# Up projection turned on VectorE in 32x32 blocks and regrouped by transfers, in place of TensorE transposes

## The chip, the cores and the metric

The kernel runs on one core of a Trainium2 chip. The metric is the time of one execution in device microseconds (us). Engines are named as in the profile: PE is TensorE (matrix products), PEld its weight load, DVE VectorE, ACT ScalarE, POOL GpSimd, SP SyncE, which only issues transfers here.

## The reference, cut to what matters

One decoder layer on 256 tokens of width 2048 in float32: parallel mixers, cross attention, and at its end a gated MLP with a causal convolution of width 3 over the tokens, then a last norm. The change touches only the MLP's first half:

```python
def causal_depthwise_conv(u, w, bias):      # per column c: y[s] = w0 u[s-2] + w1 u[s-1] + w2 u[s] + bias
    ...
def conv_ffn(h, w_up, conv_w, conv_b, w_down):
    u = causal_depthwise_conv(h @ w_up, conv_w, conv_b)
    gate, val = u[..., :D_FF], u[..., D_FF:]
    return (jax.nn.silu(gate) * val) @ w_down      # D_FF = 5632
```

## The kernel before

**Products.** Activations are held transposed and split into a high and a low part, and so are the weights. `product` computes one unit, 512 columns of x @ w for both blocks of 128 tokens, into two PSUM tiles. Weights come in transfers of 1 MB (four 128-row blocks) that SP issues into three buffers. Each is worked off in two half blocks of 256 rows: ACT casts the half block to its high part (`_hi`, L162), DVE subtracts for the low part (`_lo`, L163), and PE runs 12 matmuls of 128x512 (two row blocks, two token blocks, three terms: L168 hi x hi, L169 hi x lo, L170 lo x hi). There are three buffers each for the high and low parts, so the cast of a half block waits for the matmuls of the third half block before it. A unit of the up projection (2048 rows) is eight half blocks, 96 matmuls. After each half block `tick` lets waiting tasks go on: a task is a generator, started by `spawn(gen, delay)`, which yields the number of half blocks to let pass.

**Up stage.** 22 units, each with 256 gate and 256 value columns. After a unit ACT takes the two PSUM tiles to SBUF, scaled by the norm factor of each token (L588, `zu`). Two half blocks later `gated` runs: for the gate and for the value part PE transposes four 128x128 blocks into a PSUM tile (L562, `uT`), eight in all for a unit; for each of the four 128-column blocks ACT makes the tap of the token itself and the bias (L568) and DVE adds the other two taps (L570, L572); then a sigmoid (L576), two multiplications (L577, L578) and the split into the tile `gT` (L117, L118) that the down projection reads. Tiles that live long (`x2T`, `xr`, `gT`) share a pool of 34 buffers (`b4`).

**Order.** The code is emitted in the order of the loops, and a scheduler puts the instructions of PE, ACT, DVE and POOL in order, each engine's list being fixed when the kernel is built; SP's list stays as written. Each engine works its list off strictly in order. In the up stage POOL has nothing to do.

Of the kernel before, what the change touches and what calls it, by code (L numbers as in the profile page):

```python
# [16 lines left out]
P = 128  # L17
S = 256          # tokens
NT = S // P      # token blocks
D = 2048  # L20
KD = D // P      # 128-row blocks of the model width
FF = 5632
KF = FF // P
U = 512          # columns of one product unit
KB = 4           # 128-row blocks per weight transfer
# [6 lines left out]
# columns of the packed per-partition parameters  # L32
# [13 lines left out]
def hybrid_layer(ctx: ExitStack, tc: tile.TileContext, x, xT, mem, memT, gmix, par, gfin,  # L46
# [28 lines left out]
    # additive masks of the diagonal blocks: [q, k] -> 0 where k <= q (k < q), else NEG  # L75
# [8 lines left out]
    # Work that is emitted between the products: generators that yield the number of  # L84
    # half blocks of weights to let pass before they go on.
# [27 lines left out]
    def split(dst, src, gains=None):  # L113
        """dst[:, 0] + dst[:, 1] = src, or src * gain, in two parts of 12 bits.
        dst [P, 2, 2, S], src [P, 2, S]; gains: a [P, 1] column per 128-row block."""
        if gains is None:
            nc.scalar.copy(out=dst[:, 0], in_=src)  # L117
            nc.vector.tensor_tensor(out=dst[:, 1], in0=src, in1=dst[:, 0].bitcast(F32),  # L118
                                    op=ALU.subtract)
            return  # L120
        for j in range(2):
            nc.scalar.activation(out=dst[:, 0, j], in_=src[:, j], func=AF.Copy, scale=gains[j])
            nc.vector.scalar_tensor_tensor(out=dst[:, 1, j], in0=src[:, j], scalar=gains[j],
                                           in1=dst[:, 0, j].bitcast(F32),
                                           op0=ALU.mult, op1=ALU.subtract)

    def transposed(dst, src, n, name, gains=None):
        """dst: act tiles of the 4 row blocks n*4.. of the transpose; src [P, NT, U]."""
        for h in range(2):
            pt = sm_tile(f"{name}_tp").rearrange("p (j s) -> p j s", j=2)  # L130
            for j in range(2):
                for t in range(NT):
                    c = (2 * h + j) * P
                    nc.tensor.transpose(out=pt[:, j, t * P:(t + 1) * P],
                                        in_=src[:, t, c:c + P], identity=ident)
            k0 = 4 * n + 2 * h
            dst[k0 // 2] = act_tile(f"{name}_{h}")
            split(dst[k0 // 2], pt, None if gains is None else [gains(k0), gains(k0 + 1)])
        yield 0
# [5 lines left out]
    def rstd(ss, n, width, name):  # L145
        """(sum over the last axis of ss [P, n, m] / width + EPS) ** -0.5 -> [P, n]"""
        tot = st.tile([P, n], F32, name=f"{name}_t", tag="st_t")
        nc.vector.tensor_reduce(out=tot, in_=ss, op=ALU.add, axis=AX)
        nc.vector.tensor_scalar(out=tot, in0=tot, scalar1=1.0 / width, scalar2=EPS,
                                op0=ALU.mult, op1=ALU.add)  # L150
        r = st.tile([P, n], F32, name=name, tag=name, bufs=1)
        nc.gpsimd.tensor_tensor(out=r, in0=tot, in1=mhalf[:, :n], op=ALU.pow)
        return r
# [12 lines left out]
    def mm3(out, a, b, start=True, stop=True):  # L166
        """out (+)= (a[0] + a[1]).T @ (b[0] + b[1]) without the product of the two low parts."""
        nc.tensor.matmul(out, lhsT=a[0], rhs=b[0], start=start, stop=False)  # L168
        nc.tensor.matmul(out, lhsT=a[0], rhs=b[1], start=False, stop=False)  # L169
        nc.tensor.matmul(out, lhsT=a[1], rhs=b[0], start=False, stop=stop)  # L170
# [6 lines left out]
    def product(xs, w, u, kt_n, name, pieces=None, before=None, heap=False):  # L177
        """x @ w[:, unit u] for both token blocks -> two PSUM tiles [P, U].
        pieces: 128-row blocks per transfer; before(kt): called ahead of the transfer from kt on."""
        ps = [ps_mm.tile([P, U], F32, tag="mm", name=f"{name}_mm{t}") for t in range(NT)]  # L180
        k0 = 0
        for n in pieces or [KB] * (kt_n // KB):
            if before:
                before(k0)
            if heap:
                raw = chunk_tile(f"{name}_raw", [P, 2, U])[:, 0:n, :]
            else:
                raw = wr_p.tile([P, KB, U], F32, tag="raw", name=f"{name}_raw")[:, 0:n, :]
            k4 = k0 % KB
            nc.sync.dma_start(out=raw, in_=w[u, k0 // KB].rearrange("p (k c) -> p k c", k=KB)[:, k4:k4 + n])  # L190
            for h in range(0, n, 2):
                m = min(2, n - h)
                hi, lo = split_w(raw[:, h:h + m, :], m,
                                 ws_p.tile([P, 2, U], F32R, tag="whi", name=f"{name}_hi"),
                                 ws_p.tile([P, 2, U], F32R, tag="wlo", name=f"{name}_lo"))
                for j in range(m):
                    kt = k0 + h + j
                    for t in range(NT):
                        multiply(ps[t], xs, hi, lo, kt, j, t, kt == kt_n - 1)
                if (k0 + h) % 2 == 0 or m == 1 and kt % 2:  # L200
                    tick()
            k0 += n
        return ps

    def load_split(src, gains, i, name):
        """Split act tile i of a transposed input [P, KD, S] in DRAM, scaled by gains."""
# [27 lines left out]
    def proj_T2(ps, r, name):  # L234
        """Evacuate a unit scaled by r and transpose it: act tiles of heads 0, 1 and 2, 3."""
# [7 lines left out]
    def proj_T(ps, r, name, rotate=False):  # L243
        """Evacuate a unit scaled by r and transpose it: [P (dim), 4 (head), S]."""
# [21 lines left out]
    def proj_n(ps, r, name):  # L266
        """Evacuate a unit scaled by r: [P (token), NT, U]."""
# [5 lines left out]
    def attn_T(a, name):  # L273
        """Causal weights of one head [q block][P, K] -> [P (key), 3 * P]:
        keys 0 for both query blocks, then keys 1 for query block 1."""
# [8 lines left out]
    # differential attention  # L284
    oaT = [None] * 4

    def diff_head(h):
        qT, kT, v, hh = qa[h // 4], ka[h // 4], va[h // 4], h % 4
        # scores of the two maps, in a bank each: query block 0 in 0:P, query block 1 in P:3 * P
# [62 lines left out]
    # stick-breaking attention, two heads at a time  # L352
    obT = [None] * 4

    def stick_pair(g):
        aw = [[], []]
        for i in range(NT):
# [14 lines left out]
            # softplus(z) = max(z, 0) + ln(1 + exp(-|z|)), zero where masked  # L372
# [27 lines left out]
    # the input projection in units; the attention of a group of heads runs between the products  # L400
# [21 lines left out]
    # lam = exp(q1.k1) - exp(q2.k2) + LAM_INIT, negated, on all partitions  # L422
# [33 lines left out]
    # branch projections, gated and merged  # L456
# [18 lines left out]
    # output projection and residual  # L475
# [77 lines left out]
    gT = [None] * (KF // 2)  # L553

    def gated(i, z):
        us = []
        for part in range(2):          # gate, value
            pt = sm_tile("uT").rearrange("p (j s) -> p j s", j=2)
            for j in range(2):
                for t in range(NT):  # L560
                    c = (2 * part + j) * P
                    nc.tensor.transpose(out=pt[:, j, t * P:(t + 1) * P], in_=z[t][:, c:c + P],  # L562
                                        identity=ident)
            u = wk.tile([P, 2, S], F32, tag="w2", name="u")
            for j in range(2):
                f = part * KF + 2 * i + j
                tap = lambda k: col("cw", k * 2 * KF + f)
                nc.scalar.activation(out=u[:, j], in_=pt[:, j], func=AF.Identity, scale=tap(2),  # L568
                                     bias=col("cb", f))
                nc.vector.scalar_tensor_tensor(out=u[:, j, 1:], in0=pt[:, j, 0:S - 1], scalar=tap(1),  # L570
                                               in1=u[:, j, 1:], op0=ALU.mult, op1=ALU.add)
                nc.vector.scalar_tensor_tensor(out=u[:, j, 2:], in0=pt[:, j, 0:S - 2], scalar=tap(0),  # L572
# [11 lines left out]
    for i in range(KF // 2):  # L584
        ps = product(x2T, w_up, i, KD, f"up{i}")
        z = [wk.tile([P, U], F32, tag="w2", name=f"zu{t}") for t in range(NT)]
        for t in range(NT):
            nc.scalar.activation(out=z[t], in_=ps[t], func=AF.Copy, scale=r2[:, t:t + 1])  # L588
        spawn(gated(i, z), 2)
# [16 lines left out]
    def finish(ps, t):  # L606
        """The last unit's residual, the norm and the store of token block t."""
# [17 lines left out]
    # last unit: token block 0 runs ahead of token block 1, so that its end overlaps products  # L625
# [23 lines left out]
def _weight(w, np):  # L649
    """[K, N] -> [N / U, K / (KB * P), P, KB * U]: one contiguous transfer per block."""  # L650
# [5 lines left out]
def _tokens(a, np):  # L656
    """[S, D] -> [D / U, P, NT, U]"""
# [3 lines left out]
def _features(a, np):  # L661
    """[S, D] -> [P, KD, S]"""
# [49 lines left out]
```

## Time and profile before

| | |
|---|---|
| median of 3 runs | 1521.09 us (1521.03 to 1521.51) |
| span of the profiled execution, first to last instruction | 1518.9 us |
| PE busy | 1503.4 us (99%), granted clock 0.998 |
| DVE, ACT, POOL busy | 896.7 us (59%), 784.7 us (52%), 53.7 us (4%) |
| 16 DMA engines | 54.5% for the weights' queue |
| up stage | from about 771 to 1269 us |

The execution that was profiled has no time of its own beside its span; 2.2 us of the median lie outside the span. A matmul's row gives 389 ns, but matmuls are pipelined, and what one costs in a row of them is the distance of two starts, 0.23 us. A group's idle time is the time its engine stood still just before it, with what ended that.

### The profile page before, as it was taken

To read this page: it belongs to the slowest core of one execution; us is meant where nothing else is said; L and a number is where in the kernel's file an instruction comes from. 1 tells how busy PE (TensorE), PEld (TensorE's weight loads), DVE (VectorE), ACT (ScalarE), POOL (GpSimd) and SP (SyncE) were. 2 spreads that over 40 slices of the span, in tenths; PEclk is the share of its full clock that TensorE was granted. 3 is DMA by queue.
4 is the path that set the end of the run, shared out by engine and by line. 5 is a ranking of instruction groups with operands and counts; after the bars stand their busy time and mean duration, and the time that the engine had idled before them with its cause. 6 is when DMAs were issued, how large, how long until landed. Compare 5 with 4: busy or idle time off the path is not lost.

```text
span 1518.9 us, 17599 instructions
## 1 busy us (share of the span) xinstructions
PE 1503.4 (99%) x6904; PEld 1243.2 (82%) x6904; DVE 896.7 (59%) x1131; ACT 784.7 (52%) x1074; POOL 53.7 (4%) x72
## 2 busy tenths in 40 slices
PE   8999999999999999999999999999999999999997
PEld 6878788888888888888888888888888888888886
DVE  5575666564444565664666667666666666444562
ACT  6454555465555344664565555555555555344441
POOL 0202000000000010000000000000000000000010
PEclk9999999999999999999999999999999999999999
DMA  9544444445555556755355555555555555655561
GB/s 349 187 159 152 162 166 167 167 166 194 194 194 193 183 193 246 265 197 192 139 191 174 189 194 178 183 194 185 179 191 192 174 190 192 222 194 192 197 230 73
DMA packets 44003, 287.78 MB, mean 189 GB/s; under 512 B 5008, under 2 KB 5008, under 8 KB 11152
## 3 DMA queue, kind: packets, MB, share of 16 engines
q1 hardware_dynamic: 43488, 286.13, 54.5%
q8 instruction: 54, 0.88, 0.2%
q10 hardware_dynamic: 432, 0.53, 0.1%
q14 instruction: 29, 0.24, 0.0%
HBM read 284.54 MB, written 2.10 MB: 189 GB/s over the span
## 4 chain that ended last, share of the span: by engine, by line
PE 98%; issue 1%; DMA 0%; DVE 0%; ACT 0%; SPq 0%; POOLq 0%; POOL 0%; DVEq 0%
PE up_mm L170 11%; PE up_mm L169 11%; PE up_mm L168 11%; PE dn_mm L168 5%; PE dn_mm L170 5%; PE dn_mm L169 5%; PE g_mm L168 4%; PE g_mm L169 4%; PE g_mm L170 4%; PE wo_mm L170 2%; PE wo_mm L168 2%; PE wo_mm L169 2%; PE uT L562 1%; PE va_mm L169 1%; PE qb_mm L169 1%; PE qb_mm L168 1%
## 5 line engine op out<-in xcount | busy, mean ns | idle before, releaser
L163 DVE TENSOR_TENSOR up_lo<-up_raw,up_hi 128x1024 fp32r<-128x1024 f32 x176 | 215.7, 1226 | 170.3 <-ACT up_hi L162 167.8
L162 ACT CAST up_hi<-up_raw 128x1024 fp32r<-128x1024 f32 x176 | 185.5, 1054 | 197.5 <-PE up_mm L170 176.5
L170 PE MATMUL up_mm<-up_hi,x2T 128*128 128x512 f32 x704 | 274.1, 389 | 0.0
L169 PE MATMUL up_mm<-up_lo,x2T 128*128 128x512 f32 x704 | 274.0, 389 | 0.0
L168 PE MATMUL up_mm<-up_hi,x2T 128*128 128x512 f32 x704 | 254.8, 392 | 0.0
L163 DVE TENSOR_TENSOR dn_lo<-dn_raw,dn_hi 128x1024 fp32r<-128x1024 f32 x88 | 109.9, 1253 | 101.0 <-ACT dn_hi L162 95.7
L170 PEld LDWEIGHTS up_mm<-up_hi,x2T 128*128 128x128 f32 x704 | 132.2, 188 | 27.4
L169 PEld LDWEIGHTS up_mm<-up_lo,x2T 128*128 128x128 f32 x704 | 132.3, 188 | 26.7
L168 PEld LDWEIGHTS up_mm<-up_hi,x2T 128*128 128x128 f32 x704 | 132.2, 188 | 26.6
L162 ACT CAST dn_hi<-dn_raw 128x1024 fp32r<-128x1024 f32 x88 | 92.0, 1056 | 118.0 <-PE dn_mm L170 103.7
L170 PE MATMUL dn_mm<-dn_hi,gT 128*128 128x512 f32 x352 | 136.9, 389 | 0.0
L169 PE MATMUL dn_mm<-dn_lo,gT 128*128 128x512 f32 x352 | 136.9, 389 | 0.0
L163 DVE TENSOR_TENSOR g_lo<-g_raw,g_hi 128x1024 fp32r<-128x1024 f32 x64 | 78.4, 1225 | 83.8 <-ACT g_hi L162 83.8
L168 PE MATMUL dn_mm<-dn_hi,gT 128*128 128x512 f32 x352 | 126.3, 389 | 0.0
L162 ACT CAST g_hi<-g_raw 128x1024 fp32r<-128x1024 f32 x64 | 67.3, 1053 | 73.4 <-PE g_mm L170 70.2
L169 PE MATMUL g_mm<-g_lo,hT 128*128 128x512 f32 x256 | 100.0, 391 | 0.0
L170 PE MATMUL g_mm<-g_hi,hT 128*128 128x512 f32 x256 | 99.8, 390 | 0.0
L168 PE MATMUL g_mm<-g_hi,hT 128*128 128x512 f32 x256 | 90.7, 391 | 0.0
L170 PEld LDWEIGHTS dn_mm<-dn_hi,gT 128*128 128x128 f32 x352 | 66.1, 188 | 13.8
L169 PEld LDWEIGHTS dn_mm<-dn_lo,gT 128*128 128x128 f32 x352 | 66.1, 188 | 13.7
L168 PEld LDWEIGHTS dn_mm<-dn_hi,gT 128*128 128x128 f32 x352 | 66.1, 188 | 13.6
L170 PEld LDWEIGHTS g_mm<-g_hi,hT 128*128 128x128 f32 x256 | 48.1, 188 | 10.0
(301 smaller groups left out, 2664.5 us busy)
## 6 DMA issues: line engine op xcount, KB each, us to landing
up_raw<-in_w_up SPq DMA_DIRECT2D x88, 1024.0 KB, 4.9
dn_raw<-in_w_dn SPq DMA_DIRECT2D x44, 1024.0 KB, 4.9
g_raw<-in_w_in SPq DMA_DIRECT2D x32, 1024.0 KB, 5.0
wo_raw<-in_w_out SPq DMA_DIRECT2D x16, 1024.0 KB, 5.0
ka_raw<-in_w_in SPq DMA_DIRECT2D x8, 1024.0 KB, 6.1
va_raw<-in_w_in SPq DMA_DIRECT2D x8, 1024.0 KB, 5.0
qb_raw<-in_w_in SPq DMA_DIRECT2D x8, 1024.0 KB, 4.9
kb_raw<-in_w_in SPq DMA_DIRECT2D x8, 1024.0 KB, 4.9
```

Of the source, the lines that this page charges most:

```text
L162: nc.scalar.copy(out=hi, in_=src)
L163: nc.vector.tensor_tensor(out=lo, in0=src, in1=hi.bitcast(F32), op=ALU.subtract)
L168: nc.tensor.matmul(out, lhsT=a[0], rhs=b[0], start=start, stop=False)
L169: nc.tensor.matmul(out, lhsT=a[0], rhs=b[1], start=False, stop=False)
L170: nc.tensor.matmul(out, lhsT=a[1], rhs=b[0], start=False, stop=stop)
L562: nc.tensor.transpose(out=pt[:, j, t * P:(t + 1) * P], in_=z[t][:, c:c + P], identity=ident)
```

## The change

ACT now scales a unit in place in PSUM (L603 of the new file). DVE then turns each of the two tiles of 128x512 from PSUM into the SBUF tile `up_blk` (L129): every block of 32x32 is transposed in its place, so that a row within each 32 partitions is right, but the 4x4 grid of such blocks inside each 128x128 is not. Sixteen transfers per unit, issued from POOL's queue (L138), carry block row a, block column b to its place in `uT`, now an SBUF tile. The convolution waits in the task list for eleven half blocks after the transfers are emitted, and reads `uT` from SBUF. PE's eight transposes per unit are gone. The new file has its comments cut, and its lines have other numbers: L179 and L180 are the casts and low parts (before L162, L163), L583, L585, L587 the taps (before L568, L570, L572).

```diff
+    def turn(blk, src, t):
+
+        nc.vector.transpose(out=blk[:, :, t * P:(t + 1) * P], in_=src.rearrange("p (f c) -> p f c", c=P))
+
+    def regroup(dst, blk):
+
+
+        q = P // 4
+        d, s = (v.rearrange("p f (t c) -> p (f t) c", t=NT) for v in (dst, blk))
+        for a in range(4):
+            for b in range(4):
+                nc.gpsimd.dma_start(out=d[b * q:(b + 1) * q, :, a * q:(a + 1) * q],
+                                  in_=s[a * q:(a + 1) * q, :, b * q:(b + 1) * q])
+
+    def flip_tile(name):
+        return chunk_tile(f"{name}_blk", [P, U // P, S])
...
-    def gated(i, z):
+    def gated(i, blk):
+        uT = chunk_tile("uT", [P, U // P, S])
+        regroup(uT, blk)
+        yield 11
         us = []
-        for part in range(2):          # gate, value
-            pt = sm_tile("uT").rearrange("p (j s) -> p j s", j=2)
-            for j in range(2):
-                for t in range(NT):
-                    c = (2 * part + j) * P
-                    nc.tensor.transpose(out=pt[:, j, t * P:(t + 1) * P], in_=z[t][:, c:c + P],
-                                        identity=ident)
+        for part in range(2):
             u = wk.tile([P, 2, S], F32, tag="w2", name="u")
             for j in range(2):
                 f = part * KF + 2 * i + j
+                z = uT[:, 2 * part + j]
                 tap = lambda k: col("cw", k * 2 * KF + f)
-                nc.scalar.activation(out=u[:, j], in_=pt[:, j], func=AF.Identity, scale=tap(2),
+                nc.scalar.activation(out=u[:, j], in_=z, func=AF.Identity, scale=tap(2),
                                      bias=col("cb", f))
...
         ps = product(x2T, w_up, i, KD, f"up{i}")
-        z = [wk.tile([P, U], F32, tag="w2", name=f"zu{t}") for t in range(NT)]
-        for t in range(NT):
-            nc.scalar.activation(out=z[t], in_=ps[t], func=AF.Copy, scale=r2[:, t:t + 1])
-        spawn(gated(i, z), 2)
+        blk = flip_tile(f"up{i}")
+        for t in range(NT):
+            nc.scalar.activation(out=ps[t], in_=ps[t], func=AF.Copy, scale=r2[:, t:t + 1])
+            turn(blk, ps[t], t)
+        spawn(gated(i, blk), 1)
```

The lists of three engines, in the up stage. ACT before, from the scaling of one unit (`zu`) to that of the next:

```order
L588 ACTIVATE zu_6377<-up_mm_6208,r_6044 128x512
L588 ACTIVATE zu_6378<-up_mm_6209,r_6044 128x512
L162 CAST up_hi<-up_raw 128x1024 x3
L568 ACTIVATE u<-uT,pc 128x256 x2
L162 CAST up_hi<-up_raw 128x1024
L568 ACTIVATE u<-uT,pc 128x256 x2
L162 CAST up_hi<-up_raw 128x1024
L576 ACTIVATE sg<-u 128x512
L162 CAST up_hi<-up_raw 128x1024
L117 CAST gT_6445<-sg 128x512
L162 CAST up_hi<-up_raw 128x1024 x2
L588 ACTIVATE zu_6550<-up_mm_6381,r_6044 128x512
```

ACT now, from the scaling of the first unit over that of the second (`up_mm_6209`, `up_mm_6210`) to the third and the taps that follow it:

```order
L603 ACTIVATE up_mm_6047<-up_mm_6047,r_6044 128x512
L179 CAST up_hi<-up_raw 128x1024 x8
L583 ACTIVATE u<-uT,pc 128x256 x2
L603 ACTIVATE up_mm_6209<-up_mm_6209,r_6044 128x512
L583 ACTIVATE u<-uT,pc 128x256 x2
L603 ACTIVATE up_mm_6210<-up_mm_6210,r_6044 128x512
L179 CAST up_hi<-up_raw 128x1024
...
L603 ACTIVATE up_mm_6370<-up_mm_6370,r_6044 128x512
L179 CAST up_hi<-up_raw 128x1024
L583 ACTIVATE u<-uT,pc 128x256 x4
L179 CAST up_hi<-up_raw 128x1024 x2
```

The taps of a unit stood in the middle of the next unit, spread between its casts. They now stand at the next unit's end: for every second unit (the first, third and so on) two of them ahead of the next unit's scaling and two between its halves, for the others behind the scaling and one cast. This alternation goes on through all 22 units. The first of the four taps waits for all sixteen transfers of its unit.

DVE now, at the end of the second unit, where its two turns (L129) stand between the taps of the first:

```order
L180 TENSOR_TENSOR up_lo<-up_raw,up_hi 128x1024 x8
L585 SCALAR_TENSOR_TENSOR u<-uT,pc,u 128x255 x2
L587 SCALAR_TENSOR_TENSOR u<-uT,pc,u 128x254 x2
L129 STREAM_TRANSPOSE up_blk<-up_mm_6209 128x4x128
L585 SCALAR_TENSOR_TENSOR u<-uT,pc,u 128x255 x2
L129 STREAM_TRANSPOSE up_blk<-up_mm_6210 128x4x128
L587 SCALAR_TENSOR_TENSOR u<-uT,pc,u 128x254 x2
L180 TENSOR_TENSOR up_lo<-up_raw,up_hi 128x1024
```

Before, DVE had four taps, a low part and four taps in the middle of a unit; now eight taps and two turns stand together ahead of the low part of a unit's third half block. POOL's list gains one row between its work for `r2` and that of the down projection:

```order
L169 TENSOR_TENSOR r_6044<-r_t,mhalf 128x2
L138 DMA uT<-up_blk 32x8x32 x352
L617 TENSOR_TENSOR xr_4477<-xr_4477,gf_10425 128x512 x2
```

All 352 transfers (22 x 16) are on this one queue. The first of a unit waits for DVE's turns, and each waits until the eighth before it has landed.

## Rows read from the trace of the kernel before

**Rows 1.** Page, part 4: chain that ended last, shares of the span.

```profile
PE 98%; issue 1%; DMA 0%; DVE 0%; ACT 0%; SPq 0%; POOLq 0%; POOL 0%; DVEq 0%
PE up_mm L170 11%; PE up_mm L169 11%; PE up_mm L168 11%; PE dn_mm L168 5%; PE dn_mm L170 5%; PE dn_mm L169 5%; PE g_mm L168 4%; PE g_mm L169 4%; PE g_mm L170 4%; PE wo_mm L170 2%; PE wo_mm L168 2%; PE wo_mm L169 2%; PE uT L562 1%; PE va_mm 
```

**Rows 2.** Page, part 1: busy us, share of the span, instructions.

```profile
PE 1503.4 (99%) x6904; PEld 1243.2 (82%) x6904; DVE 896.7 (59%) x1131; ACT 784.7 (52%) x1074; POOL 53.7 (4%) x72
```

**Rows 3.** Windows, up stage: busy us, count, clock, DMA share, GB/s.

```profile
772.00:1270.00 498.00, 498.00 (x2288) 414.41 (x2287) 323.75 (x417) 278.65 (x357) 0.69 (x1) 1.00 0.54 186
```

**Rows 4.** Timeline of PE: start us, us, instructions; a unit apart.

```profile
1000.09 0.39 PE L170 MATMUL up_mm<-up_hi,x2T 128*128 128x512 f32 x1
...
1002.81 0.39 PE L170 MATMUL up_mm<-up_hi,x2T 128*128 128x512 f32 x1
1003.05 1.03 PE L562 MATMUL uT<-ident,zu 128*128 128x128 f32 x8
1003.84 0.48 PE L168 MATMUL up_mm<-up_hi,x2T 128*128 128x512 f32 x1
...
1025.70 1.03 PE L562 MATMUL uT<-ident,zu 128*128 128x128 f32 x8
```

**Rows 5.** Tile uT: durations in ns, first and last start.

```profile
L562 PE MATMUL uT<-ident,zu x176: 270/272/273, 799.2 to 1275.6; 128*128 128x128 f32 x176
L568 ACT ACTIVATE u<-uT,pc x88: 552/556/563, 800.3 to 1280.1; 128x256 f32<-128x256 f32 x88
```

**Rows 6.** Timeline at a unit's end, ACT, DVE and PE.

```profile
1017.79 1.06 ACT L162 CAST up_hi<-up_raw 128x1024 fp32r<-128x1024 f32 x1 [1.72 <-PE up_mm L170]
...
1018.88 1.23 DVE L163 TENSOR_TENSOR up_lo<-up_raw,up_hi 128x1024 fp32r<-128x1024 f32 x1 [1.55 <-ACT up_hi L162]
...
1019.77 1.37 ACT L588 ACTIVATE zu<-up_mm,r 128x512 f32<-128x512 f32 x2 [0.93 <-PE up_mm L170]
...
1020.03 0.39 PE L170 MATMUL up_mm<-up_hi,x2T 128*128 128x512 f32 x1
...
1020.25 0.62 PE L168 MATMUL up_mm<-up_hi,x2T 128*128 128x512 f32 x2
...
1021.04 1.04 ACT L162 CAST up_hi<-up_raw 128x1024 fp32r<-128x1024 f32 x1
...
1022.12 1.23 DVE L163 TENSOR_TENSOR up_lo<-up_raw,up_hi 128x1024 fp32r<-128x1024 f32 x1 [2.01 <-ACT up_hi L162]
...
1023.17 1.06 ACT L162 CAST up_hi<-up_raw 128x1024 fp32r<-128x1024 f32 x1 [1.09 <-PE up_mm L170]
```

**Rows 7.** Timeline of DVE: the taps of one part.

```profile
1005.47 0.87 DVE L570 SCALAR_TENSOR_TENSOR u<-uT,pc,u 128x255 f32<-128x255 f32 x2
1006.25 0.86 DVE L572 SCALAR_TENSOR_TENSOR u<-uT,pc,u 128x254 f32<-128x254 f32 x2
```

**Rows 8.** Waits of ACT in the up stage: us, times, longest.

```profile
ACT up_hi L162 <- PE up_mm L170: 176.2, 127, 1.7
```

**Rows 9.** Groups by form, DVE: count, busy us, mean ns, idle.

```profile
L123 DVE SCALAR_TENSOR_TENSOR memT<-memT_raw,pc,memT 128x256 fp32r<-128x256 f32 x16 | 7.1, 481 | 0.0
...
L260 DVE COPY qaT<-qaT_tp 128x512 f32<-128x512 f32 x4 | 2.7, 688 | 2.0 <-PE qaT_tp L258 2.0
```

**Rows 10.** Groups by form, POOL.

```profile
L467 POOL TENSOR_TENSOR gate<-gate,gate 128x512 f32<-128x512 f32 x8 | 14.1, 1789 | 358.5 <-issue 358.5
...
L227 POOL TENSOR_TENSOR rope_a<-qaT_z,pc 128x128 f32<-128x128 f32 x4 | 4.2, 1054 | 12.9 <-ACT qaT_z L249 12.7
```

**Rows 11.** Timeline of SP: its first issue.

```profile
0.74 0.39 SPq L208 DMA_DIRECT2D hT_raw<-in_xT  x1
```

**Rows 12.** DMA issues: KB each, median us to landing.

```profile
up_raw<-in_w_up SPq DMA_DIRECT2D x88, 1024.0 KB, 4.9
...
out<-xr SPq DMA_DIRECT2D x6, 256.0 KB, 2.3
```

**Rows 13.** DMA, first 4 us: the queue that moves 64-byte rows.

```profile
q10 hardware_dynamic: 144, 0.01, 2.4%
```

More of the change, by code (lines that the diff above doesn't have):

```diff
@@ L566, in gated @@
                 f = part * KF + 2 * i + j
+                z = uT[:, 2 * part + j]
                 tap = lambda k: col("cw", k * 2 * KF + f)
-                nc.scalar.activation(out=u[:, j], in_=pt[:, j], func=AF.Identity, scale=tap(2),
+                nc.scalar.activation(out=u[:, j], in_=z, func=AF.Identity, scale=tap(2),
                                      bias=col("cb", f))
-                nc.vector.scalar_tensor_tensor(out=u[:, j, 1:], in0=pt[:, j, 0:S - 1], scalar=tap(1),
+                nc.vector.scalar_tensor_tensor(out=u[:, j, 1:], in0=z[:, 0:S - 1], scalar=tap(1),
                                                in1=u[:, j, 1:], op0=ALU.mult, op1=ALU.add)
-                nc.vector.scalar_tensor_tensor(out=u[:, j, 2:], in0=pt[:, j, 0:S - 2], scalar=tap(0),
+                nc.vector.scalar_tensor_tensor(out=u[:, j, 2:], in0=z[:, 0:S - 2], scalar=tap(0),
                                                in1=u[:, j, 2:], op0=ALU.mult, op1=ALU.add)
```

## The prediction

> **What bounds the kernel now.** I read the chain of waits first: it is almost wholly PE's own work, and PE's transposes into `uT` stand on it by themselves with 1% [rows 1]. Busy times next: PE 99%, the others far from full [rows 2]. The window over the up stage shows no gap on PE, full granted clock, and DMA engines 54% busy [rows 3]. So in this stage time is what PE has to do, as long as nothing that feeds it is late. PE's timeline gives the prices: twelve matmul starts lie between 1000.09 and 1002.81, 2.72 us for a half block, 0.2267 each; the eight transposes of two successive units start at 1003.05 and 1025.70, 22.65 us apart [rows 4]. 96 matmuls make 21.76 us, so the transposes take 0.88 us of each unit.
>
> **What goes.** 176 transposes [rows 5], 22 x 0.88 = 19.3 us, all on the path. Nothing on PE takes their place. The sum is made against the profiled span, 1518.9 us, which becomes 1499.6; the median of the runs is 2.2 us above the span, so 1521.1 becomes 1501.8 if all else stays hidden.
>
> **What comes on ACT and DVE.** The scaling is the same instruction with PSUM as target; no row shows ACT writing there, and I keep 0.69 us each (1.37 for two [rows 6]). The taps read SBUF in place of PSUM; the same form from SBUF takes 481 ns on DVE [rows 9], the price it has from PSUM, so nothing there. The turn is not in the trace. Its bounds are a pass over half the columns, 0.48 us [rows 9], and over twice as many, 1.23 us [rows 6]; a copy of 128x512 out of PSUM took 0.69 us [rows 9], and I take that, the nearest row: 1.4 us per unit on an engine that is busy 324 of 498 us [rows 3]. In total that is hidden; what matters is where it stands.
>
> The place is a unit's end. Count from E, the first matmul of the next unit, 1020.25 in the timeline [rows 6]. The cast of that unit's second half block runs from E-2.46 to E-1.40, its low part to E-0.14; the scaling starts at E-0.48 and both halves take 1.37. PE wants the third half block at E+5.44, its low part one matmul later, at E+5.67. Before, that low part was done at 1023.35, E+3.1, so 2.6 us were spare. Now, in the list of every second unit, DVE has four taps, a turn, two taps, a turn and two taps ahead of it. Four taps took 1.64 us [rows 7], 0.41 each. From E-0.14: 1.64 + 0.69 + 0.82 + 0.69 + 0.82 + 1.23 = 5.89, done at E+5.75. That uses the whole margin and 0.1 us, for 11 such places 1 us; a turn of 1.23 us, or a dearer write to PSUM by as much, would make it 13 us. For the other units the low part stands ahead of the taps, and a margin of over 1 us stays.
>
> **The wait that comes.** At these 11 places the first tap on ACT waits for all sixteen transfers, and behind it in ACT's list stand the scaling of the unit just ended and the cast of the third half block; behind the first tap on DVE the turns and that low part. To lose nothing the tap must start by about E-0.75 (DVE's first tap 0.6 us later). The turns that feed these transfers stood at the unit end before, in the form without taps ahead: scaling done at E+0.89, second turn about E+1.65. One unit later makes 21.76 - 0.75 - 1.65 = 19.4 us from the last turn to the landing of the last transfer. At the alternate places the turns end later (E+3.7), but the taps wait behind scaling and a cast, and up to E+3.8 is free: 21.76 - 3.7 + 3.8 = 21.9 us. If the transfers take C us, then, each pair of units loses C - 19.4 where that is positive (a wait at the second place only widens the first place's window), 11 times. Eleven half blocks, 29.9 us, are thus not what the transfers get: the fixed lists give them 19.4.
>
> C is sixteen issues on POOL and the last one's way. For the way I take the smallest landing in the trace, 2.3 us for 256 KB [rows 12]. One issue from POOL's queue stands nowhere in the trace. Lower end: SP's issue of a transfer of 128 rows, 0.39 us [rows 11], C = 8.5. Upper end: POOL's longest instruction, 1.79 us [rows 10], C = 30.9. Between them I take POOL's row that also steps through short strided pieces, `rope_a`, 1.05 us [rows 10]: each transfer here is 32 partitions x 8 pieces of 128 bytes. C = 16 x 1.05 + 2.3 = 19.1, inside 19.4. That is the narrow place of this forecast. No other work on POOL is queued in the stage (one instruction of 0.69 us at its start [rows 3]); the wait for the eighth transfer before does not bind, since eight issues take 8.4 us and a landing 2.3.
>
> **The DMA engines.** Per unit they get 4096 pieces, 256 per engine, beside 0.54 x 22.65 = 12.2 us of weights. The one row with such small pieces is the load of 64-byte rows: 2.4% of 16 engines in 4 us for 144 packets [rows 13], 11 ns each. At one to two times that, 2.7 to 5.5 us, at most 17.7 of 21.76. Weights will land later than 4.9 us [rows 12], but a buffer that comes free is wanted again only five half blocks later, 13.6 us less 2.3 of cast and low part, so 6 us are to spare, and ACT's casts wait for PE and not for data [rows 8].
>
> The Trainium skill ("DMA: Bandwidth & Descriptors", Specifications) says that a transfer needs pieces of 512 bytes or more for full rate, and that below this the engine reads, modifies and writes; the row of 64-byte packets at 11 ns does not show such a penalty, though it reads from HBM, and the rule is weighed below as a rival.
>
> **Rivals.**
> A: issuing is dearer, and the unit's end waits. For: 352 issues on one queue, a pattern of 256 pieces each, twice the 128 rows of SP's issue. Against: SP's 0.39 us, and POOL's small instructions. It decides from C = 19.4 on, 1.07 us an issue; the gain is gone at C = 19.4 + 19.3/11 = 21.2, 1.18 us an issue. At 1.4 us, C = 24.7: 11 x 5.3 = 58, 1501.8 + 58 = 1560. At 1.79 us, 28.6 us of issue per unit is above the average period, and the queue itself is the bound: 22 x (28.6 - 21.76) = 150, 1652.
> B: small pieces fill the DMA engines. Take each piece as 512 bytes moved twice: weights cost 16 x 12.2 us for 8192 pieces of 512 bytes, 24 ns, doubled 48. Then 256 x 48 ns = 12.2 us more per engine, 24.4 per unit against 21.76: 22 x 2.7 = 59, so 1561. Against it stands the 11 ns row [rows 13].
> C: the transfers follow one another instead of overlapping, each to its landing: 16 x 2.3 = 37 us per unit [rows 12], 22 x 15 = 335, about 1837. Against: the waits in POOL's list go back eight transfers. The Trainium skill ("DMA: Bandwidth & Descriptors", Anatomy of one DMA, the gpsimd path) gives such a transfer about 2.0 us fixed plus its bytes over 436 GB/s, an estimate of 2.1 us here and 33 us for sixteen if none overlapped.
> D: no change: A between 1.15 and 1.2 us an issue, the saving eaten by the wait.
>
> **Chances.** A measurement of this kernel tells 0.2%, 3 us, from no change. Forecast, all of the saving or up to 6 us less, 0.48; A in part, or dear turns, 1508 to 1518, 0.09; D 0.06; A slower, 0.27; B 0.06; C 0.04. So faster 0.57, same 0.06, slower 0.37. The forecast is 1501.8 and the 1 us at the unit ends: 1502.5, its own range 1500 to 1508. The range that leaves out about 2 in 10 reaches into A up to 1.43 us an issue and takes in B's price: 1500 to 1567.
>
> **What would show it.** Right: units 21.8 us apart on PE, no idle time before the matmuls of the third half block, sixteen issues in under 17 us on POOL's queue, `uT` landed before ACT reaches the first tap, the turns at 0.7 us. Wrong by A: ACT's first tap waiting on `uT`, PE idle at every second unit's third half block, the chain running over POOL's queue and the transfers. Wrong by B: DMA share near 1.0 and casts waiting for weights. Wrong from the start would be a turn far over 0.7 us, or matmuls dearer than 0.2267 without the transposes between them.

## The result, and the profile after

The changed kernel takes 1500.95 us (median of four, 1500.69 to 1501.38), the kernel before 1521.06 beside it: ratio 0.9869, 95% interval 0.9854 to 0.9884. The forecast was 1502.5. The profiled span went from 1518.9 to 1499.6 us, by the 19.3 us of PE transposes that the sum took off; the medians lie 20.1 us apart.

The chain that ended last and PE's busy time are as they were, without the transposes' entry [rows 1, 2]; the other engines have more to do in a shorter span. Page, parts 1 and 4:

```profile
PE 1484.7 (99%) x6728; PEld 1225.4 (82%) x6728; DVE 919.5 (61%) x1175; ACT 781.6 (52%) x1074; POOL 256.2 (17%) x424
...
PE 98%; issue 1%; DMA 1%; DVE 0%; ACT 0%; SPq 0%; POOLq 0%; POOL 0%; DVEq 0%
```

The stage's window (busy us of PE, PEld, DVE, ACT, POOL; then clock, DMA share, GB/s), against [rows 3], and everything that PE waited for in the whole run:

```profile
772.00:1250.00 478.00, 478.00 (x2115) 395.88 (x2114) 340.50 (x449) 273.42 (x351) 193.97 (x337) 1.00 0.66 217
```

```profile
engine line waited for: us in total, times, longest us
PE qa_mm L185 <- ACT qa_hi L179: 6.0, 1, 6.0
PE qa_mm L186 <- DVE qa_lo L180: 0.4, 1, 0.4
```

PE waits twice, at the start of the run, and never in the up stage, at full granted clock. POOL went from 0.69 us to 194 us there and nobody waits for it. What the new work costs, from the tiles `uT` and `up_blk` (min/median/max ns) and from the page's DMA parts (packets, MB, share; and KB, us to landing):

```profile
L138 POOL DMA_DIRECT2D uT<-up_blk x352: 582/582/775, 797.1 to 1265.3; - x176
L583 ACT ACTIVATE u<-uT,pc x88: 587/592/601, 814.9 to 1276.1; 128x256 f32<-128x256 f32 x88
L587 DVE SCALAR_TENSOR_TENSOR u<-uT,pc,u x88: 437/477/484, 817.0 to 1279.8; 128x254 f32<-128x254 f32 x88
...
DMA to landing us min/median/max: 1.8/3.8/6.5
```

```profile
L129 DVE STREAM_TRANSPOSE up_blk<-up_mm x44: 695/716/718, 795.0 to 1254.4; 128x512 f32<-128x512 f32 x44
```

```profile
q0 software_dynamic: 11264, 11.56, 3.0%
...
up_raw<-in_w_up SPq DMA_DIRECT2D x88, 1024.0 KB, 5.2
...
uT<-up_blk POOLq DMA_DIRECT2D x352, 32.0 KB, 3.8
```

The two kinds of unit's end, in time order from the timelines of ACT, DVE and POOL (start, us, instruction; in brackets idle time before it); before, see [rows 6]:

```profile
989.15 1.23 DVE L180 TENSOR_TENSOR up_lo<-up_raw,up_hi 128x1024 fp32r<-128x1024 f32 x1 [1.45 <-ACT up_hi L179]
990.10 0.66 ACT L603 ACTIVATE up_mm<-up_mm,r 128x512 f32<-128x512 f32 x1
990.29 0.87 DVE L585 SCALAR_TENSOR_TENSOR u<-uT,pc,u 128x255 f32<-128x255 f32 x2
...
993.25 0.71 DVE L129 STREAM_TRANSPOSE up_blk<-up_mm 128x512 f32<-128x512 f32 x1
994.26 8.04 POOL L138 DMA_DIRECT2D uT<-up_blk  x14 [14.35 <-DVE up_blk L129]
994.64 1.22 DVE L180 TENSOR_TENSOR up_lo<-up_raw,up_hi 128x1024 fp32r<-128x1024 f32 x1
...
1003.72 1.16 POOL L138 DMA_DIRECT2D uT<-up_blk  x2 [1.42 <-DMA uT<-up_blk]
...
1011.86 1.34 ACT L603 ACTIVATE up_mm<-up_mm,r 128x512 f32<-128x512 f32 x2 [0.99 <-PE up_mm L187]
1012.56 1.40 DVE L129 STREAM_TRANSPOSE up_blk<-up_mm 128x512 f32<-128x512 f32 x2 [0.42 <-ACT up_mm L603]
1014.07 2.08 ACT L583 ACTIVATE u<-uT,pc 128x256 f32<-128x256 f32 x4
...
1018.42 5.74 POOL L138 DMA_DIRECT2D uT<-up_blk  x10 [0.73 <-issue]
...
1032.54 1.09 ACT L583 ACTIVATE u<-uT,pc 128x256 f32<-128x256 f32 x2
```

The scalings of the two units start at 990.10 and 1011.86, 21.76 us apart: PE's matmuls and nothing else. The first unit's turns end at 993.96, its sixteen issues at 1004.88, ACT's first tap reads the result at 1014.07. The second's end at 1013.96 and 1024.16, the tap is at 1032.54. The way counts from the start of an issue. For the last issue of each (tile `uT`, windows 1004.31 to 1004.8 and 1023.6 to 1024.1) it is longer than the median of 3.8 us:

```profile
DMA to landing us min/median/max: 4.2/4.2/4.2
```

```profile
DMA to landing us min/median/max: 6.1/6.1/6.1
```

So the data are there at 1008.5 and 1029.7, 5.6 us and 2.8 us ahead of the taps. Over all 22 units the last landing is 2.8 to 6.8 us ahead of the first tap.

### The profile page after: what moved, and what is told of

Same layout as the page of the kernel before. It is cut to its first block, busy times and chain, and to the rows that moved or that the text cites. A ratio compares the mean times of both kernels' runs of the same rounds, so it can differ in the third digit from the quotient of the medians.

```text
span 1499.6 us, 17849 instructions
## 1 busy us (share of the span) xinstructions
PE 1484.7 (99%) x6728; PEld 1225.4 (82%) x6728; DVE 919.5 (61%) x1175; ACT 781.6 (52%) x1074; POOL 256.2 (17%) x424
## 3 DMA queue, kind: packets, MB, share of 16 engines
q1 hardware_dynamic: 43488, 286.13, 54.8%
q0 software_dynamic: 11264, 11.56, 3.0%
## 4 chain that ended last, share of the span: by engine, by line
PE 98%; issue 1%; DMA 1%; DVE 0%; ACT 0%; SPq 0%; POOLq 0%; POOL 0%; DVEq 0%
PE up_mm L185 11%; PE up_mm L187 11%; PE up_mm L186 11%; PE dn_mm L186 5%; PE dn_mm L187 5%; PE dn_mm L185 5%; PE g_mm L185 4%; PE g_mm L187 4%; PE g_mm L186 4%; PE wo_mm L187 2%; PE wo_mm L186 2%; PE wo_mm L185 2%; PE va_mm L186 1%; PE qb_mm L186 1%; PE qb_mm L185 1%; PE kb_mm L187 1%
## 5 line engine op out<-in xcount | busy, mean ns | idle before, releaser
L180 DVE TENSOR_TENSOR up_lo<-up_raw,up_hi 128x1024 fp32r<-128x1024 f32 x176 | 214.5, 1223 | 130.7 <-ACT up_hi L179 130.7
L179 ACT CAST up_hi<-up_raw 128x1024 fp32r<-128x1024 f32 x176 | 184.9, 1050 | 192.2 <-PE up_mm L187 176.0
L187 PE MATMUL up_mm<-up_hi,x2T 128*128 128x512 f32 x704 | 273.9, 389 | 0.0
L138 POOL DMA_DIRECT2D uT<-up_blk x352 | 202.5, 583 | 287.8 <-DVE up_blk L129 169.1
L185 PE MATMUL up_mm<-up_hi,x2T 128*128 128x512 f32 x704 | 246.1, 389 | 0.0
L180 DVE TENSOR_TENSOR dn_lo<-dn_raw,dn_hi 128x1024 fp32r<-128x1024 f32 x88 | 109.8, 1253 | 94.9 <-ACT dn_hi L179 89.8
L179 ACT CAST dn_hi<-dn_raw 128x1024 fp32r<-128x1024 f32 x88 | 91.8, 1054 | 115.2 <-PE dn_mm L187 99.9
L180 DVE TENSOR_TENSOR g_lo<-g_raw,g_hi 128x1024 fp32r<-128x1024 f32 x64 | 78.4, 1225 | 83.9 <-ACT g_hi L179 83.9
L179 ACT CAST g_hi<-g_raw 128x1024 fp32r<-128x1024 f32 x64 | 67.2, 1051 | 73.5 <-PE g_mm L187 70.3
```

The source lines that it names most:

```text
L138: nc.gpsimd.dma_start(out=d[b * q:(b + 1) * q, :, a * q:(a + 1) * q], in_=s[a * q:(a + 1) * q, :, b * q:(b + 1) * q])
L179: nc.scalar.copy(out=hi, in_=src)
L180: nc.vector.tensor_tensor(out=lo, in0=src, in1=hi.bitcast(F32), op=ALU.subtract)
```

## The experiments

Ratios are to the kernel before, measured beside each run (medians 1521.0 to 1521.2). All start from the changed kernel (e5 is told by its difference from e2); none leaves work out.

**r1: the PE time back.** Eight transposes of a constant per unit on PE, read by nobody.

```
         regroup(uT, blk)
-        yield 11
+        yield 1
+        for part in range(2):
+            pt = sm_tile("idle")
+            for j in range(4):
+                nc.tensor.transpose(out=pt[:, j * P:(j + 1) * P], in_=ident, identity=ident)
+        yield 10
```

> The changed kernel, and besides eight transposes per unit again on PE, of the constant identity into a PSUM tile that nobody reads, at the second half block as before. They wait for no data. Theory (the gain is PE's time for the transposes, 0.88 us a unit, and nothing else): 1500.9 + 19.3 = 1520.3 us. Rival (the gain came from the wait of the transposes for the scaled tiles, or from freeing PSUM, ACT or DVE in the middle of a unit): PE would take the constant transposes at less cost and the time stays at 1501 to 1510 us.

1522.91 us, ratio 1.0012 (1.0002 to 1.0021): the whole gain is gone with PE's time, though the transfers and the turns stay. It costs 2.6 us more than asked; these transposes wait for nothing, and the trace has them between 785 and 973 in groups of one to nine, not in eights. By the starts of the matmuls around them these groups take 20.0 us in all, where the 22 groups of eight in the kernel before take 19.4, so the grouping accounts for 0.6 us; the other 2 were not followed up.

**r2: three half blocks in place of eleven** (`yield 11` becomes `yield 3`).

> The changed kernel with the convolution three half blocks after the transfers in place of eleven, which changes the lists little, since the scheduler places the taps about a unit later by itself. Theory (the sixteen transfers land some 13 us after the turns, in the 19 that the lists leave): 1501 us, within 2. Rival (eleven is what hides the transfers, and earlier taps wait for them): each unit waits some microseconds, 1520 us or more.

1645.15 us, ratio 1.0816 (1.0799 to 1.0832). My theory that the eleven does not matter fell. The trace does not show a wait for transfers (waits of PE first; then the timelines of ACT, DVE and PE):

```profile
PE up_mm L185 <- ACT gT L117: 90.5, 17, 6.0
```

```profile
859.15 1.34 ACT L603 ACTIVATE up_mm<-up_mm,r 128x512 f32<-128x512 f32 x2 [0.94 <-PE up_mm L187]
...
879.82 2.07 ACT L583 ACTIVATE u<-uT,pc 128x256 f32<-128x256 f32 x4
881.10 0.87 DVE L585 SCALAR_TENSOR_TENSOR u<-uT,pc,u 128x255 f32<-128x255 f32 x2
...
881.16 0.39 PE L187 MATMUL up_mm<-up_hi,x2T 128*128 128x512 f32 x1
...
886.72 1.31 DVE L129 STREAM_TRANSPOSE up_blk<-up_mm 128x512 f32<-128x512 f32 x2
887.57 0.77 PE L185 MATMUL up_mm<-up_hi,x2T 128*128 128x512 f32 x1 [6.02 <-ACT gT L117]
```

A unit scaled at 859.15 is turned only at 886.72, 27 us later. Until then it holds its two PSUM tiles. There are four, so the unit after next, due at 881.39, starts when the first of the turns is through; the releaser named in brackets, a cast that ended last by the profile, is not what it needs. ACT's taps at 879.82 show no idle time before them: their data were there. After the pause the clock is at the lower level (windows of r2):

```profile
888.00:890.00 2.00, 2.00 (x6) 1.52 (x6) 0.59 (x2) 0.00 (x0) 1.41 (x3) 0.50 0.11 25
...
892.00:896.00 4.00, 4.00 (x19) 3.33 (x18) 0.27 (x1) 1.05 (x1) 3.90 (x8) 1.00 0.27 57
```

0.50 is the 1.2 GHz level, six matmuls in 2 us; in the second window they are back at 19 in 4. With 144.2 us over 18 units the price is 8.0 us for each late unit, of which the pause is up to 6.

Why the turns are late stands in the built instruction lists. Counted in low parts of `up` weights that DVE has ahead of an instruction, after the own unit's last one:

| kernel | second turn of units 1 to 22 | units at 9 or more |
|---|---|---|
| changed, eleven | 2 in 21 units | 0 |
| r2, three | 2, 5, 9, then 11 in 17 | 18 |
| r6, eight | 2 in five, 5, 7, 10, then 11 in 12 | 13 |
| r7, eight, copied | as r6 up to 10, then 13 to 27 in 11, then 16 | 13, but its scaling only 5 |

Not in the table are the last units, behind which few or none of the stage's low parts are left: unit 21 has 8 and unit 22 has 0 in r2, r6 and r7, and unit 22 has 0 in the changed kernel. My reading of the lists is this. The builder keeps DVE's turns of a unit behind taps that were emitted earlier, and it places the taps by its own idea of when transfers land. With three half blocks the taps of a unit are emitted before the next unit's turns, and in r2's list (DVE's order in its trace) these turns stand one to three low parts behind the first of those taps: turn, transfers, taps and the next turn make one loop, which slips by two to four low parts per unit until the PSUM tiles run out.

This does not explain everything. With eight half blocks, as with eleven, the taps are emitted after the next unit's turns. In r6 it is then the taps of the unit before last behind which the turns come to stand (units 6, 7 and 8 behind the taps of 4, 5 and 6), and those taps slip from the first units on, at 10, 13, 16, 18 and 20 low parts, while with eleven they stay at 10 and 11. Why the builder lets them slip with eight and not with eleven is not shown.

**r6 and r7: eight half blocks; and eight with the scaled tile copied.** Both to test that reading: r6 is `yield 8`; r7 adds a PSUM tile of its own to the turn, so that the matmul's tile is free after the scaling.

```
         for t in range(NT):
-            nc.scalar.activation(out=ps[t], in_=ps[t], func=AF.Copy, scale=r2[:, t:t + 1])
-            turn(blk, ps[t], t)
+            z = sm_tile("zu")
+            nc.scalar.activation(out=z, in_=ps[t], func=AF.Copy, scale=r2[:, t:t + 1])
+            turn(blk, z, t)
```

> Eight half blocks in place of eleven; nothing else is edited. Counted in DVE's low parts of the up weights after a unit's own last one, the changed kernel's list has the second turn of every unit at 2 and its taps at 10 or 11. With three half blocks the list has the turns at 11 for 18 of the 22 units, and the run cost 144 us more than the changed kernel, 8.0 us for each of these. With eight it has them at 10 or 11 for 13 units, at 2 to 7 for the first seven. Theory 1, a turn that comes so late holds the unit's two PSUM tiles past the first matmul of the next unit but one: 1501 + 13 x 8.0 = 1605 us, with about 13 pauses of PE, none before the eighth unit. Theory 2, the transfers need the half blocks as time: here the taps stand at 13 to 26, later than in the changed kernel, so 1501.

> Eight half blocks as in the run beside it, and the scaling writes into another PSUM tile (one of the four that the transposes used), from which the turn reads; so the matmul's own tile is free once it is scaled, however late the turn is. Turns are as late as in the run beside it or later (at 10 to 27 low parts for 13 units), but the scaling itself stands at 2 for the first 13 units, and at 10 or 11 for five. Theory 1, the held PSUM tile: 1501 + 5 x 8.0 = 1541, with about five pauses at the end of the stage. Theory 3, late turns or late taps cost by themselves (DVE's order, late gated tiles): like the run beside it, 1605 or more. Theory 2: 1501.

r6: 1604.4 us, ratio 1.0549 (1.0534 to 1.0565), as theory 1 has it; time for the transfers (theory 2) is out, since the taps stand later than in the changed kernel. r7: 1571.1, ratio 1.0329 (1.0312 to 1.0346), between theories 1 and 3. PE's waits, r6 then r7:

```profile
PE up_mm L185 <- ACT gT L117: 56.1, 12, 4.7
PE dn_mm L185 <- ACT gT L117: 7.6, 2, 4.7
```

```profile
PE dn_mm L185 <- ACT gT L117: 19.7, 4, 7.7
PE up_mm L185 <- ACT zu L604: 18.7, 4, 5.0
...
PE dn_mm L185 <- ACT zu L604: 4.3, 1, 4.3
```

r7 has the five pauses on the scaling that theory 1 asks for, none before 1130 us, with the turns as late as in r6 for 13 units: freeing the tile took the other pauses away. What I had left out are its first row's four waits: the gated tiles are so late that the down projection waits for them, 19.7 us. 1541 and 19.7 make 1561. The remaining 10 us go with the clock: all PE waits that r7 has beyond the start of the run are 46.1 us, and its mean granted clock of 0.981, against 0.999 in the changed kernel, is worth up to 28 us of 1569 (a part of the low clock lies in the waits). Together they cover the 70 us that r7 loses.

**r3 and r4: the transfers on ACT's and on SP's queue** (`nc.gpsimd.dma_start` becomes `nc.scalar` or `nc.sync`).

> The changed kernel with the sixteen transfers of a unit issued from ACT's queue. In ACT's list they stand behind the scaling and one cast. Theory (an issue holds its engine, 0.39 us each as SP's and ACT's rows of before show): from about E+2.3 to E+8.5, so that the fourth half block's cast ends at E+9.6 and its low part at E+10.7, wanted at E+8.4; 2.3 us a unit, 22 x 2.3 = 51, so 1552 us; at 0.33 us an issue 1530. Rival (issuing costs the engine nothing that PE waits for): 1501 us.

> The changed kernel with the transfers issued from SP's queue, whose list stays as written: a unit's sixteen stand behind the next unit's first weight transfer and ahead of its second. Theory (the queue that waits for the turns holds what is behind it): the second weight transfer is issued at about E+8 and lands at E+13, PE wants its low part at E+5.7: some 9 us a unit, 22 x 9 = 200, about 1700 us. Rival (three weight buffers cover it): 1501 us.

r3: 1695.0 us, ratio 1.1137 (1.1119 to 1.1156). r4: 1848.8, a single run. The direction was right, the sizes not. ACT's timeline in r3:

```profile
918.69 1.04 ACT L179 CAST up_hi<-up_raw 128x1024 fp32r<-128x1024 f32 x1
919.55 11.52 ACTq L138 DMA_DIRECT2D uT<-up_blk  x16
931.17 1.04 ACT L179 CAST up_hi<-up_raw 128x1024 fp32r<-128x1024 f32 x1 [11.44 <-DMA uT<-up_blk]
```

ACT issues for 11.5 us and casts no weights meanwhile. PE's next matmul that wants them starts at 932.27 after 6.05 us. That happens once a unit (117.1 us, 21 times), and 194 us over 22 units is 8.8 each: a pause of 5.6, and matmuls at the lower clock behind it. Here the twelve from 932.27 on take until 937.93, 5.7 us where 2.7 is usual, about 0.4 of it a wait for the low part, at a granted clock of 0.50 (window 932.5 to 937.5). The list has changed too: the taps stand at 6 low parts and not at 10 or 11. In r4 the loss is larger for a reason that is not the queue alone: in its lists the taps stand at 2 low parts, right behind the turns, so ACT waits for the landing with the casts behind it (ACT, then PE):

```profile
921.74 2.08 ACT L583 ACTIVATE u<-uT,pc 128x256 f32<-128x256 f32 x4 [12.22 <-DMA uT<-up_blk]
```

```profile
926.96 1.22 PE L185 MATMUL up_mm<-up_hi,x2T 128*128 128x512 f32 x2 [13.24 <-ACT up_hi L179]
```

So r4 tells the price of taps placed too early, 16 us a unit, and not that of SP's queue by itself.

The Trainium skill ("DMA: Bandwidth & Descriptors", Issuing engines are not separate DMA queues) says that issuing from several engines at once only saves the time that it takes to issue, which is usually small beside the transfer. Here that time is what decides: in r3 it is 11.5 us of a unit of 21.76.

**r5: 64 transfers per unit.** Each of the sixteen is cut in four, `for h in range(4)` over two of its eight pieces.

> The changed kernel with each transfer cut into four, 64 per unit on POOL's queue with 64 pieces of 128 bytes each; bytes and pieces in sum are the same. The lists have the taps some three units later. Theory (POOL pays 0.58 us per issue whatever the pieces, and the queue is the bound from 21.8 us a unit on): 64 x 0.58 = 37 us a unit, 22 x 15.4 = 339, about 1840 us. Rival (POOL pays per piece): 64 issues take what sixteen took, 9.3 us, and the time stays at 1501 us. Between them, a fixed part of 0.45 us: 29 us a unit, about 1655.

1856.2 us, a single run. Tile `uT`, and POOL's busy time as the fifth in a window of 740 us:

```profile
L140 POOL DMA_DIRECT2D uT<-up_blk x1408: 533/533/732, 797.3 to 1646.9; - x176
```

```profile
860.00:1600.00 740.00, 486.81 (x1959) 393.44 (x1958) 336.49 (x423) 264.32 (x323) 645.10 (x1227) 0.83 0.41 133
```

An issue costs 0.53 us with 64 pieces and 0.58 with 256: the price hangs on the transfer, hardly on its pieces. 64 x 0.533 = 34.1 us is above the unit's 21.76, and POOL is busy 87% of the window; 22 x 12.4 = 272 of the 355 us follow from that. The rest is not separated: its lists also have the turns at 11 in 18 units, and ACT's taps wait for transfers for 118.1 us.

**e1 to e3: the same treatment for other transposes.** e1 gives it to the eight q and k units, e2 to the four of x1T (their split six half blocks later), e3 to six, four and three of q/k, x1T and mT.

> The changed kernel, and the same turn and sixteen transfers for the eight units of q and k of the two mixers too (64 transposes less on PE, POOL has the rotary work as well). Theory (0.87 us of PE's time per eight transposes comes off wherever the transfers are hidden): 8 x 0.87 = 7.0, so 1494 us. Rival (the heads want q and k sooner than the transfers land, PE waits): between 1497 and above 1501.

> The changed kernel, and the turn and transfers for the four transposed units that cross attention reads, which are wanted a unit of the memory's projection later. Theory: 4 x 0.87 = 3.5 us off, 1497.4 us. Rival (the last of them lands late): 1501 or more.

> The changed kernel, and the turn and transfers for six of the eight units of q and k (not the first of the first mixer), for the four units of cross attention and the first three of the merged branches. Theory: 6 x 0.87 + 4 x 0.87 + 3 x 0.87 = 11.3 us off, 1489.6 us. Rival (one of these places waits): part of that is given back, 1493 to 1501.

All missed: 1510.88 us (ratio 0.9931, 0.9914 to 0.9948), 1505.71 (0.9898, 0.9884 to 0.9913) and 1516.95 (0.9971, 0.9960 to 0.9982), all slower than the changed kernel. In e1 POOL has the rotations of q and k to do as well, and PE waits in the attention, where the changed kernel has no wait (two of six such rows):

```profile
PE oa L356 <- DVE da_aT L313: 4.7, 2, 2.8
PE oaT L374 <- DVE o L369: 2.6, 1, 2.6
```

These six come to 13.3 us, against 7.0 gained; which of the late tiles starts them was not followed up. In e3 such rows come to 17.9 us, against 11.3, the largest (7.2 us) where e2 has its loss. In e2 the place is plain (ACT, then PE):

```profile
616.35 1.05 ACT L192 CAST wo_hi<-wo_raw 128x1024 fp32r<-128x1024 f32 x1 [1.67 <-PE wo_mm L200]
622.17 1.71 ACT L122 ACTIVATE x1T<-x1T_tr,pc 128x256 fp32r<-128x256 f32 x4 [4.77 <-DMA x1T_tr<-x1T_blk]
```

```profile
627.54 0.73 PE L198 MATMUL wo_mm<-wo_hi,mT 128*128 128x512 f32 x2 [3.07 <-ACT wo_hi L192]
```

ACT stands 4.77 us before data that are still on their way, and the next weights' cast stands behind it.

**e5 and e6: later.** e5 is e2 with `yield 9` for `yield 6`; e6 turns three of the four units of mT as well.

> The four units of x1T turned by DVE as in the experiment e2, but their casts nine half blocks later in place of six. In e2 ACT waited 4.8 us for the transfers of the first unit, the cast of the next weights stood behind it, and PE waited 4.9 and 1.1 us in this stage. If that wait was the loss, it is gone and the 4 x 0.88 us of PE transposes remain as gain: 1501.0 - 3.5 = 1497.5. If moving transposes off PE is worth nothing in this stage (another wait takes their place), 1501 to 1506.

> The same with three of the four units of mT turned as well, nine half blocks later. 7 x 0.88 = 6.2 us of PE transposes gone: 1494.8 if all stays hidden. POOL adds the gates in that stage (3.5 us per unit) and now issues 16 transfers (9.3 us) there, of 22 us; rival: the gates stand behind the transfers on POOL and PE waits for the last unit's transposes, 2.8 us as in e3, 1498 or more.

e5: 1497.17 us (0.9843, 0.9828 to 0.9858); e6: 1495.21 (0.9831, 0.9816 to 0.9845), 26 us below the kernel before and the best of all. In e5 PE's only waits are those at the start of the run; in e6 there is one more:

```profile
PE wo_mm L199 <- DVE wo_lo L193: 0.8, 1, 0.8
```

Each 0.88 us of transposes taken off PE is a gain of 0.8 to 0.95 us (3.8 us for four, 5.7 for seven), once nothing waits for the transfers.

## Why the prediction was right

1. **PE's time on the path.** 22 x 0.88 = 19.3 was asked, and r1 gives the gain back, e5 and e6 repeat it elsewhere. That the spans differ by just 19.3 is partly luck: in the profiled execution the first matmul of the up stage starts at 771.96, before at 770.94, in code that the change leaves alone, and from there to the end it is 20.3 us shorter. The medians say 20.1, r1 costs 22.0. The price holds to within 15%, and the 0.8 us by which the medians exceed it are not accounted for.
2. **The turn and the taps.** The turn takes 0.716 us for an assumed 0.69, the taps 477 ns for 481. ACT's tap from SBUF is 592 ns where 556 stood before [rows 5], an item that I had at nothing; 88 of them are 3 us of an engine with room.
3. **The narrow unit's end.** I had the low part of the third half block done at E+5.75, and 1 us lost over eleven places. With E = 990.58 it is done at 995.86, E+5.28: DVE's row of taps and turns began 0.15 us earlier and ran 0.3 shorter. I had also read the need too early, one matmul behind the first, E+5.67. PE's list has two matmuls with the high part ahead, and wants the low part at 996.48, E+5.90:

```profile
996.02 0.62 PE L185 MATMUL up_mm<-up_hi,x2T 128*128 128x512 f32 x2
996.48 0.39 PE L186 MATMUL up_mm<-up_lo,x2T 128*128 128x512 f32 x1
```

So even E+5.75 would have cost nothing, and 0.6 us are to spare. The forecast is also added up wrongly: 1501.8 and 1 are 1502.8 and not 1502.5. Of the 1.85 us by which that is high, 1 us is this term, 0.4 the time outside the span (1.8 us in the profiled run, not 2.2), and 0.4 the profiled run's distance from the median (1501.38 for 1500.95).
4. **The window for the transfers.** The step was right in kind, and its windows nearly (20.1 and 18.6 us between last turn and first tap). Mis-sized was the term that I called the narrow place: an issue took 0.583 us, not 1.05. `rope_a` steps through short pieces as an instruction of compute; an issue hardly pays by its pieces, as r5 shows, and SP's 0.39 us [rows 11] was the nearer row. That 1.05 fell below the limit of 1.07 was a choice between rows and no knowledge. The way was longer, 3.8 us in the median for 2.3 and 6.1 for the last transfer of the second unit shown; with that way the limit would have been an estimated (19.4 - 6.1) / 16 = 0.83 us an issue. And the wait for the eighth transfer before, which I had excluded, does bind: 16.0 us in 16 places, 1.4 us in the first unit shown. All together the trace has 13.3 to 15.8 us from the last turn to the last landing, against 19.1, so the margin is at least 3.6 us where I had 0.3, and rival A, which got 0.27 and with B's price the upper part of the range, did not come.
5. **The DMA engines.** q0's 3.0% of 1499.6 us over 22 units is 2.0 us per engine and unit, below my 2.7 to 5.5. Rivals B (12.2) and C (one after another) are out. A transfer is 32 packets whether it has 256 pieces (11264 for 352) or 64 in r5 (45056 packets for 1408). The row of 64-byte packets did not speak against a penalty as I had it: 64 bytes in 11 ns are 6 GB/s per engine, where the weights' queue before has 22 (286.13 MB in 54.5% of 16 x 1518.9 us). The Trainium skill has the penalty for small pieces for HBM only ("DMA: Bandwidth & Descriptors", Why small descriptors are slow), and the trace agrees in the main: SBUF to SBUF, with 128-byte pieces, q0 moves 16 GB/s per engine (11.56 MB in 3.0% of 16 x 1499.6 us), three quarters of the weights' rate and far above what B took.
6. **The step that hid something.** "Eleven half blocks are thus not what the transfers get" was right, and yet I took the lists as given and never asked what they would be with another number. The eleven is worth 144 us against three, by the order of DVE's work and the PSUM tiles that this order holds.

## What to carry to other kernels

Where one engine is busy 99% of the span, price what you take off it at its full time, then look only for the instruction behind which its feeder waits. A delay written into the code can matter as order and not as time: read in the built list what stands behind what, and count the buffers held meanwhile. When a move to slower hands loses, look first whether a reader stands too early in an in-order queue: three half blocks later turned e2's loss into e5's gain.

## What the runs showed of the hardware

- Issue time on the issuing engine for the same transfer: 0.58 us on POOL, 0.62 on ACT, 0.61 on SP (medians); with a quarter of the pieces 0.53 on POOL.
- The way from issue to landing, for the same 32 KB, was 3.8 us median in the changed kernel (POOL's queue), 1.9 in r3 and r4 (ACT's and SP's), and 1.9 also in r2 and r6, which use POOL's queue. So the queue is not what makes the difference. In r2 the first three units have 3.6 to 4.0 and the others, once PE pauses, 1.8 to 1.9, save 3.6 in the last. The share of the 16 DMA engines was 0.74 while the changed kernel's first unit shown was under way (994 to 1006), 0.26 in r2 (1094 to 1106) and 0.45 in r3 (919.5 to 931). That the other traffic lengthens the way is the likely cause; no run varies it alone.
- A DVE turn of 128x512 in 32x32 blocks out of PSUM takes 0.716 us, a plain copy of that shape 0.688 [rows 9].
- After a pause of 6 us on PE the granted clock stood at 0.50 for the first matmuls. With it a pause is dearer than its length: r3 pays 8.8 us a unit for 5.6 us of waiting.
